# The MLP of an encoder layer: earlier loads for the background sums, one more set of output buffers, a finish with other spacing

## The chip, the core and the metric

One core of one Trainium2 chip runs the whole layer. The metric is the device time of one execution in microseconds (us); for the kernel before, the median of three runs is 3302.6 us (3301.38 to 3305.57). The engines are TensorE (PE), VectorE (DVE), ScalarE (ACT), GpSimd (POOL) and SyncE (SP), which issues nearly all DMAs of this part.

## The reference, cut to what matters

The layer works on `x` of 2048 tokens by 1024 channels, all in float32: an SSD (Mamba-2) head group and a windowed attention group, mixed by `w_out`, and then the MLP, which is the part that the change touches:

```python
x = x + rmsnorm(mix, norm_mix_post[i])
h = rmsnorm(x, norm_mlp_pre[i])                             # 2048 x 1024
f = jnp.square(jax.nn.relu(h @ w_up[i])) @ w_down[i]        # 1024 -> 4096 -> 1024
x = x + rmsnorm(f, norm_mlp_post[i])
```

## The kernel before

**Precision.** A float32 product is made of three matmuls: each operand is split into a high part (ACT rounds a copy) and a low part (DVE or POOL subtracts the copy), and hi*hi, hi*lo and lo*hi are summed in PSUM. A weight or input that reaches PE thus costs one ACT copy and one subtraction.

**Fast products.** The two large products of the MLP use a 2x2 block scheme with seven block products in place of eight. For this the operands are needed in linear combinations: sums of input blocks, sums of weight blocks, and sums of the outputs of the first product, which are the inputs of the second.

**Up.** The tokens go in two halves (`hf` 0 and 1). Each half has 16 steps `p`; a step makes seven products (`PROD` = 1, 5, 6, 3, 7, 2, 4) of 12 matmuls of 128x512 each, into PSUM tiles psmx, psmy and psmz. Products 1, 5, 6 and 4 are copied by ACT into SBUF tiles `c` (L1083; product 4 with a ReLU, L1054), products 3, 7 and 2 are added to them by DVE (L1086). Product 3 goes on accumulating in the bank of product 5, and product 7 in that of product 6, so PE can start them only when ACT has copied the bank out. The `c` tiles have five buffers (tag "ct") for four tiles a step. At the end of a step POOL forms four more combinations (L1096, L1098, L1100, L1105) in tiles `t`, and all of it is stored to DRAM (`dop`). The last four steps of the second half store to `dff` and need no combinations.

**Inputs of up.** `up_input` loads the rows of `x2`, scales them, forms the combinations on DVE and POOL, and splits them (L1039, L1040) into tiles of the pools "u" (16) and "a" (16). For the second half it starts in step 15 of the first, each set when the set of the first half that it replaces has been used.

**Weights of down.** In the background, `w_sums` takes 16 jobs: load four tiles of `w_down` into the four buffers of the tag "nt" (L1117), four additions on POOL in place (L1121), four stores to `dws` (L1122). It starts after step 3 of the first half. The tag "nt" also holds the scratch tiles of `rnorm` and `rsqrt`, which `r2` calls at step 8 of each half, when PE has summed the squares (`ssq`).

**Down.** `down_fast` runs four quarters for the first half of the tokens and three for the second, 28 products of 12 matmuls each; the last quarter goes as an ordinary product (`down`). `down_weights` loads `wd` tiles and splits them (L1147, L1148); `down_input` brings the inputs back from `dop` through the small staging tiles "gl" (2) and "ld" (3), and splits them (L1164, L1165). The tags "ld" and "gl" also hold POOL's `t` tiles. `finals` finishes the first half of the tokens while the second runs: one `ssq` on PE for each of two column blocks, then eight times a scale, an addition and a store (L1281 to L1285).

**Order of the work.** The order on PE is the order in which the program is written: generators are interleaved by a clock `self.t` that counts matmul time, 512/2400 of a microsecond for each 128x512 matmul (17.92 units a step of up), and `yield n` means "not before n units from now". On the other engines a scheduler orders the instructions when the program is built; there the place in the program is a priority, and a tile's buffer is given out in program order.

Of the kernel before, what the change touches and what calls it, by code (L numbers as in the profile page):

```python
# [37 lines left out]
class Layer:  # L38
    def __init__(self, ctx, tc, a, out):
# [21 lines left out]
        self.d_x2 = d("dx2", [8, P, T])  # L61
        self.d_h = d("dh", [2, 8, P, 2, 2, TB])
# [901 lines left out]

    def up_weights(self):
# [11 lines left out]
        for u in range(32):  # L977
            nxt = load((u + 1) % 16) if u < 31 else None
            for m in self.PROD:
# [5 lines left out]
                w = self.wp.tile([P, 2, 4, P], F32R, tag="ws", name="ws", bufs=4)  # L985
                nc.scalar.copy(w[:, 0], x)  # L986
                self.eng("wlo").tensor_sub(w[:, 1], x, w[:, 0].bitcast(F32))  # L987
                yield w
# [8 lines left out]
    def up_input(self, hf, B):  # L997
# [5 lines left out]
        sets = ((("raw1", "u", None), ("raw2", "u", None), (1, "u", None), (5, "u", None), (6, "a", "ws10"),  # L1003
                 (3, "a", "ws10"), (7, "a", "ws11"), (2, "a", "ws11"), (4, "u", None)) if hf == 0 else
                (("raw1", "u", None), ("raw2", "u", "uA1"), (1, "u", "uA5"), (5, "a", "uA6"), (6, "a", "uA3"),
                 (3, "a", "uA7"), (7, "a", "uA2"), (2, "u", "uA4"), (4, "u", None)))
        x = {}

        def raw(b, tag):

            x[b] = []
            for i in range(4):
                t = self.unit(tag, "x2", F32)
                for k in range(2):
                    kt = 4 * k + i
                    nc.sync.dma_start(t[:, k], self.d_x2[kt, :, self.tok(hf, b - 1)])
# [7 lines left out]
        for s, tag, after in sets:  # L1024
            if after:
                yield self.until(after)
            if s in ("raw1", "raw2"):
                yield self.until(f"x2_{hf}{int(s[3]) - 1}")
# [14 lines left out]
            self.flags.add(f"B{hf}{s}")  # L1043

    def up(self, hf, p, B, ws):
# [15 lines left out]
        for m in self.PROD:  # L1061
# [16 lines left out]
            if m in (1, 5, 6, 4):  # L1078
                c[m] = self.pw.tile([P, TB], F32, tag="ct", name=f"c{m}", bufs=5)
# [28 lines left out]
    def w_sums(self):  # L1108

        nc = self.nc  # L1110
        for qt in range(4):
            for p in range(4):
                a = {}
                for i in range(2):
                    for k in range(2):
                        t = a[f"{i + 1}{k + 1}"] = self.nt("wsum")
                        nc.sync.dma_start(t.rearrange("p (k c) -> p k c", k=4), self.a["w_down"][2 * p + i, 2 * qt + k])  # L1117
                yield 6
                for m, fn, x, y, o in ((5, "tensor_add", "21", "22", "21"), (6, "tensor_sub", "21", "11", "11"),
                                       (7, "tensor_sub", "22", "11", "22"), (3, "tensor_sub", "12", "11", "12")):  # L1120
                    getattr(nc.gpsimd, fn)(a[o], a[x], a[y])  # L1121
                    nc.sync.dma_start(self.d_ws[(5, 6, 7, 3).index(m), qt, p], a[o])  # L1122
                yield 22
# [8 lines left out]
    def down_weights(self):  # L1132
        nc = self.nc
        for hf in range(2):
            for qt in range(3 if hf else 4):
                for m, ps in self.DPH:
                    for p in ps[::2]:
                        raw = self.pf.tile([P, 2, 4, P], F32, tag="f", name="wd", bufs=8)
# [6 lines left out]
                        for x in range(2):  # L1145
                            w = self.wp.tile([P, 2, 4, P], F32R, tag="ws", name="ws", bufs=4)
                            nc.scalar.copy(w[:, 0], raw[:, x])  # L1147
                            self.eng("wlo").tensor_sub(w[:, 1], raw[:, x], w[:, 0].bitcast(F32))  # L1148
                            yield w

    def down_input(self):

        nc = self.nc
        done = ["uB5", "uB6", "uB3", "uB7"]
        for hf in range(2):
            for qt in range(3 if hf else 4):
                for m in self.DIN:
                    yield self.until(done.pop(0))
                    done.append(f"D{hf}{qt}{m}")
                    B = self.B2[hf, qt, m] = []  # L1160
                    for i in range(4):
                        x = self.stage(self.d_op[hf, m - 1, 4 * qt + i], i)
                        t = self.slot("ff")
# [417 lines left out]
```

## Time and profile before

| | us |
|---|---|
| median of three runs | 3302.6 |
| the profiled execution | 3297.75 |
| its span | 3296.0 |
| PE busy in the span | 2973.0 (90%) |
| DVE, ACT, POOL busy | 2167.4, 1555.7, 1132.7 |
| DMA, mean rate | 179 GB/s |

The MLP takes the last 45% of the span. A busy PE counts its pipelined matmuls, and a stretch at the lower granted clock is also busy, so idle time of PE and its granted clock are read together. Idle time of the other engines costs nothing by itself.

### The profile page before, as it was taken

The numbers are of one execution on the slowest core, as the hardware profiler recorded it, in microseconds if no ns is written. First come the engines' busy times: TensorE is split into PE (matmuls) and PEld (weight loads), VectorE is DVE, ScalarE is ACT, GpSimd is POOL, SyncE is SP. The second block draws the span as 40 slices with busy tenths as digits, with TensorE's granted clock in tenths as the row PEclk, the third lists the DMA queues.
The fourth block names the chain that finished last, engine by engine and source line by source line (L and its number), as shares of the span: only waits on it lengthen the run. The fifth ranks groups of instructions, "written<-read, shape, count | busy, mean of one in ns | idle before, by whom it ended". The sixth has DMA issues, their size and how long they took to land. (4 is left out here: it accounts for less than half of the span.)

```text
span 3296.0 us, 40950 instructions
## 1 busy us (share of the span) xinstructions
PE 2973.0 (90%) x13560; PEld 2369.2 (72%) x13560; DVE 2167.4 (66%) x3514; ACT 1555.7 (47%) x2886; POOL 1132.7 (34%) x900
## 2 busy tenths in 40 slices
PE   7989999999998899997978779886998899988996
PEld 6878887778876666674756557764877788877886
DVE  7365555557757788859778855648564467767766
ACT  3235566667765445222132535534554554454432
POOL 4242222222233444654536555567344000020001
PEclk9999999999999999997989989988999999999998
DMA  6767544475568645655257465564445556557633
GB/s 227 238 201 202 147 126 119 125 215 136 154 210 258 194 140 157 186 172 160 88 165 242 161 229 185 210 221 171 148 165 205 188 188 201 194 178 249 193 104 97
DMA packets 422117, 589.19 MB, mean 179 GB/s; under 512 B 34704, under 2 KB 202640, under 8 KB 421904
## 3 DMA queue, kind: packets, MB, share of 16 engines
q1 hardware_dynamic: 387280, 550.90, 54.0%
q10 hardware_dynamic: 34624, 35.66, 3.1%
q8 instruction: 108, 1.77, 0.2%
q14 instruction: 105, 0.86, 0.1%
HBM read 391.77 MB, written 194.65 MB: 178 GB/s over the span
## 5 line engine op out<-in xcount | busy, mean ns | idle before, releaser
L88 PE MATMUL psg<-h,ws 128*128 128x512 f32 x1920 | 486.4, 400 | 19.3 <-ACT z L472 17.9
L88 PEld LDWEIGHTS psg<-h,ws 128*128 128x128 f32 x1920 | 356.9, 190 | 93.0 <-issue 18.6
L220 POOL TENSOR_SCALAR ws<-wr 128x512 fp32r<-128x512 f32 x184 | 126.6, 688 | 740.7 <-PE psg L88 602.3
L86 PE MATMUL psmx<-b,ws 128*128 128x512 f32 x1152 | 304.1, 415 | 41.1 <-ACT c L1083 19.4
L86 PEld LDWEIGHTS psmx<-b,ws 128*128 128x128 f32 x1152 | 229.5, 201 | 101.1 <-ACT c L1083 22.6
L223 POOL TENSOR_TENSOR ws<-wr,ws 128x512 fp32r<-128x512 f32 x184 | 250.7, 1363 | 14.7
L88 PE MATMUL psg<-hr,ws 128*128 128x512 f32 x960 | 248.6, 399 | 5.0 <-DMA hr<-dh 4.3
L779 DVE CUSTOM_DVE_ANT_0 p<-psqk,pack,sinks 128x384 f32<-128x384 f32 (+1 forms) x256 | 151.9, 596 | 139.3 <-PE psqk L88 138.6
L86 PE MATMUL psx<-ff,ws 128*128 128x512 f32 x1008 | 233.9, 392 | 7.8 <-DVE ws L1148 7.7
L88 PE MATMUL psg<-ga,ws 128*128 128x512 f32 x768 | 209.9, 426 | 26.4 <-DVE mix L895 11.8
L86 PEld LDWEIGHTS psx<-ff,ws 128*128 128x128 f32 x1008 | 190.4, 189 | 49.1 <-DVE ws L1148 9.1
L1147 ACT CAST ws<-wd 128x512 fp32r<-128x512 f32 x196 | 121.9, 623 | 215.4 <-PE psx L86 93.4
L88 PE MATMUL psg<-ya,ws 128*128 128x512 f32 x768 | 212.9, 418 | 2.0 <-DVE ya L203 1.9
L88 PEld LDWEIGHTS psg<-hr,ws 128*128 128x128 f32 x960 | 175.9, 189 | 41.7 <-DMA hr<-dh 7.1
L88 PEld LDWEIGHTS psg<-ga,ws 128*128 128x128 f32 x768 | 150.6, 201 | 75.1 <-issue 11.9
L88 PEld LDWEIGHTS psg<-ya,ws 128*128 128x128 f32 x768 | 142.0, 193 | 43.4 <-issue 15.0
L987 DVE TENSOR_TENSOR ws<-wc,ws 128x512 fp32r<-128x512 f32 x128 | 132.8, 1039 | 56.4 <-ACT ws L986 56.0
L790 ACT ACTIVATE p<-p,m 128x384 f32<-128x384 f32 (+1 forms) x256 | 150.9, 591 | 35.3 <-DVE m L785 35.1
L208 ACT CAST pt<-pspt 128x512 fp32r<-128x512 f32 x184 | 107.0, 583 | 119.2 <-PE pspt L92 103.4
L1148 DVE TENSOR_TENSOR ws<-wd,ws 128x512 fp32r<-128x512 f32 x196 | 137.1, 701 | 38.1 <-ACT ws L1147 37.8
L209 DVE TENSOR_TENSOR pt<-pspt,pt 128x512 fp32r<-128x512 f32 x184 | 125.5, 684 | 50.2 <-ACT pt L208 49.7
L88 PE MATMUL psy<-ff,ws 128*128 128x512 f32 x672 | 156.7, 390 | 1.7 <-DVE facc L1205 1.2
(246 smaller groups left out, 6455.2 us busy)
## 6 DMA issues: line engine op xcount, KB each, us to landing
stg<-dop SPq DMA_DIRECT2D x196, 256.0 KB, 3.5
wu<-w_up_dram SPq DMA_DIRECT2D x128, 256.0 KB, 3.3
wr<-w_in_dram SPq DMA_DIRECT2D x120, 256.0 KB, 2.8
dop<-c SPq DMA_DIRECT2D x112, 256.0 KB, 2.3
wd<-dws SPq DMA_DIRECT2D x56, 512.0 KB, 4.2
k<-dk SPq DMA_DIRECT2D x56, 384.0 KB, 4.8
dop<-t SPq DMA_DIRECT2D x84, 256.0 KB, 2.1
wd<-w_down_dram SPq DMA_DIRECT2D x42, 512.0 KB, 4.3
```

The costliest lines, as they stand in the source:

```text
L86: self.nc.tensor.matmul(out, lhsT, rhs, start=False, stop=stop, skip_group_check=True)
L88: self.nc.tensor.matmul(out, lhsT, rhs, start=start, stop=stop)
L208: self.nc.scalar.copy(hi, src)
L209: self.nc.vector.tensor_sub(lo, src, hi.bitcast(F32))
L220: self.nc.gpsimd.tensor_scalar(w[:, 0], raw, 1.0, 0.0, ALU.mult, ALU.add)
L223: eng.tensor_sub(w[:, 1], raw, w[:, 0].bitcast(F32))
L779: nc.vector.tensor_tensor_reduce(out=p[:, :W], in0=ps[:, :W], in1=bias, scale=1.0, scalar=self.sinks[:, hd:hd + 1], op0=ALU.add, op1=ALU.m ...
L790: nc.scalar.activation(p4[r][:, :W], p4[r][:, :W], AF.Exp, bias=m[:, 0, r:r + 1], scale=float(np.float32(SLOPES[hd])), accum_out=m[:, 2, r ...
L987: self.eng("wlo").tensor_sub(w[:, 1], x, w[:, 0].bitcast(F32))
L1147: nc.scalar.copy(w[:, 0], raw[:, x])
L1148: self.eng("wlo").tensor_sub(w[:, 1], raw[:, x], w[:, 0].bitcast(F32))
```

## The change

- `w_sums` becomes `sums`: 20 jobs in place of 16. The first four jobs load four tiles of `x2` of the second half, scale them, and store the seven inputs of the second half's up products to a new DRAM array `dxo`. Then come the 16 jobs on `w_down`. The loads of a job are written three units behind the sums of the job before, and its sums 18 units later (before: loads, 6 units, sums, 22 units).
- `up_input1` replaces `up_input` for the second half: it loads the ready inputs through the staging tiles and only splits them, from step 14 on.
- The `c` tile of product 4 goes to the tag "wr" (two buffers of the weight chunks, not in use during up); the five "ct" buffers serve the other three.
- The first four `wd` tiles go to "nt" buffers, as part of a weight stream that starts in the last step of up; `down_input` starts in step 14 with its first set in the "u" pool.
- `finals` starts 8 units later, and its elements are 7 units apart (before: 1.5). The same `yield` serves the first of the three last parts.

```diff
+    def up_input1(self, B):
+        for m, tag, after in ((1, "u", "xo"), (5, "u", "uA1"), (6, "u", "uA5"), (3, "a", "uA6"), (7, "a", "uA3"),
+                              (2, "a", "uA7"), (4, "a", "uA2")):
+            yield self.until(after)
+            B[m] = []
+            for i in range(4):
+                x = self.stage(self.d_xo[m - 1, i], i)
+                t = self.unit(tag, "b")
+                nc.scalar.copy(t[:, 0], x)
+                self.eng("flo").tensor_sub(t[:, 1], x, t[:, 0].bitcast(F32))
+                B[m].append(t)
+                yield 1.0
+            self.flags.add(f"B1{m}")
...
-                c[m] = self.pw.tile([P, TB], F32, tag="ct", name=f"c{m}", bufs=5)
+                c[m] = (self.wp.tile([P, TB], F32, tag="wr", name="c4", bufs=2) if m == 4 else
+                        self.pw.tile([P, TB], F32, tag="ct", name=f"c{m}", bufs=5))
...
+    def sums(self):
+        def load(job):
+            a = {}
+            for i in range(2):
+                for k in range(2):
+                    t = a[f"{i + 1}{k + 1}"] = self.nt("sum")
...
+        def x_sums(i, a):
+            for y, m in (("11", 1), ("12", None), ("22", 3), ("21", 2)):
+                kt = 4 * int(y[0]) - 4 + i
+                nc.vector.tensor_scalar(a[y], a[y], vec[:, kt:kt + 1], None, ALU.mult)
+                if m:
+                    nc.sync.dma_start(self.d_xo[m - 1, i], a[y])
+            t1, t2 = self.ld(name="t1"), self.gl("t2")
+            nc.gpsimd.tensor_sub(t1, a["12"], a["11"])
+            nc.sync.dma_start(self.d_xo[4, i], t1)
+            nc.gpsimd.tensor_sub(t2, a["22"], t1)
+            nc.sync.dma_start(self.d_xo[5, i], t2)
+            nc.gpsimd.tensor_sub(a["12"], a["22"], a["12"])
+            nc.sync.dma_start(self.d_xo[6, i], a["12"])
+            t4 = self.ld(name="t4")
+            nc.gpsimd.tensor_sub(t4, a["21"], t2)
+            nc.sync.dma_start(self.d_xo[3, i], t4)
...
+        jobs = [(i,) for i in range(4)] + [(qt, p) for qt in range(4) for p in range(4)]
+        a = load(jobs[0])
+        for n, job in enumerate(jobs):
+            yield 18
+            (x_sums if len(job) == 1 else w_sums)(*job, a)
+            if n == 3:
+                self.flags.add("xo")
+            elif n > 3 and job[1] == 3:
+                self.flags.add(f"sum{job[0]}")
+            if n + 1 < len(jobs):
+                yield 3
+                a = load(jobs[n + 1])
...
+                        if (hf, qt, m) == (0, 0, 1):
+                            raw = [self.nt("wd").rearrange("p (k c) -> p k c", k=4) for _ in range(2)]
+                            for x in range(2):
+                                nc.sync.dma_start(raw[x], self.a["w_down"][2 * (p + x), 0])
+                                yield self.wsplit(raw[x])
+                            continue
...
-        done = ["uB5", "uB6", "uB3", "uB7"]
+        done = [None, "uB3", "uB7", "uB2", "uB4"]
...
+        yield self.until(f"sum{qt}")
...
-            yield 0 if xs else 1.5
+            yield 0 if xs else 7
...
+                if (hf, p) == (1, 15):
+                    ws = itertools.chain(ws, self.down_weights())
...
-                if p == 15:
-                    if hf == 0:
-                        self.side(self.up_input(1, B[1]))
-                    else:
-                        self.side(self.down_input())
+                if p == 14:
+                    self.side(self.down_input() if hf else self.up_input1(B[1]))
...
-                self.side(self.finals(both, facc, facs))
+                self.side(self.finals(both, facc, facs), 8)
```

## Rows read from the trace of the kernel before

**Rows 1.** Windows: stretch, length, busy PE, PEld, DVE, ACT, POOL; PEclk, DMA, GB/s.

```profile
1821.76:1957.16 135.40, 93.54 (x341) 71.83 (x340) 94.33 (x111) 63.58 (x108) 63.20 (x41) 0.86 0.58 192
1957.16:2069.12 111.96, 103.06 (x425) 82.38 (x424) 63.84 (x70) 58.84 (x96) 57.73 (x39) 0.95 0.53 183
2069.12:2246.24 177.12, 144.49 (x590) 116.01 (x589) 96.20 (x104) 76.71 (x133) 108.27 (x74) 0.90 0.64 228
2246.24:2295.58 49.34, 28.92 (x85) 18.89 (x84) 45.70 (x35) 21.59 (x40) 44.40 (x29) 0.77 0.35 122
2295.58:2429.25 133.67, 133.67 (x590) 110.64 (x588) 81.02 (x92) 74.88 (x127) 56.40 (x39) 1.00 0.44 156
2429.25:2524.28 95.03, 82.14 (x341) 65.52 (x340) 51.13 (x60) 49.48 (x80) 47.54 (x34) 0.95 0.58 199
...
2611.54:2922.31 310.77, 307.56 (x1344) 254.04 (x1345) 212.41 (x318) 149.89 (x252) 19.14 (x14) 0.99 0.61 195
2922.31:3173.97 251.66, 236.71 (x1012) 191.87 (x1013) 184.81 (x282) 121.01 (x203) 12.17 (x8) 0.98 0.65 204
```

**Rows 2.** Timeline of PE, an undisturbed step: start, length, line, output, count.

```profile
2339.49 2.88 PE L86 MATMUL psmx<-b,ws 128*128 128x512 f32 x12
2342.21 2.88 PE L86 MATMUL psmy<-b,ws 128*128 128x512 f32 x12
```

**Rows 3.** Waits of PE, 1957 to 2246: total us, times, longest.

```profile
PE psmy L86 <- ACT c L1083: 28.6, 8, 11.8
PE psmx L86 <- DVE c L1086: 6.6, 1, 6.6
PE ssq L88 <- DMA xsld<-dxs: 3.3, 1, 3.3
```

**Rows 4.** Waits of ACT, 1957 to 2246.

```profile
ACT c L1083 <- POOL c L1100: 52.7, 9, 15.5
```

**Rows 5.** Waits of POOL, 1957 to 2246.

```profile
POOL wsum L1121 <- DMA wsum<-w_down_dram: 53.9, 7, 9.6
```

**Rows 6.** Timeline of POOL: sums of a job before and after each gap.

```profile
2001.22 6.49 POOL L1121 TENSOR_TENSOR wsum<-wsum 128x512 f32<-128x512 f32 x4 [6.56 <-DMA wsum<-w_down_dram]
...
2079.57 6.39 POOL L1121 TENSOR_TENSOR wsum<-wsum 128x512 f32<-128x512 f32 x4
...
2287.32 1.73 POOL L1121 TENSOR_TENSOR wsum<-wsum 128x512 f32<-128x512 f32 x1
...
2465.51 6.40 POOL L1121 TENSOR_TENSOR wsum<-wsum 128x512 f32<-128x512 f32 x4
```

**Rows 7.** Timeline of PE: the first `ssq` of `r2` in each half.

```profile
2053.30 1.43 PE L88 MATMUL ssq<-xsld,ones 128*128 128x512 f32 x2 [3.29 <-DMA xsld<-dxs]
...
2438.97 1.39 PE L88 MATMUL ssq<-xsld,ones 128*128 128x512 f32 x2 [2.76 <-DMA xsld<-dxs]
```

**Rows 8.** Line L1121 and loads L1117: durations ns (min/median/max); landing time.

```profile
L1121 POOL TENSOR_TENSOR wsum<-wsum x64: 1261/1622/1813, 1957.3 to 2506.5; 128x512 f32<-128x512 f32 x64
...
DMA to landing us min/median/max: 2.6/4.1/6.8
```

**Rows 9.** Subtractions on DVE: with POOL at work (L1040), without (L1165).

```profile
L1040 DVE TENSOR_TENSOR b<-x,b x14: 678/1748/1780, 2238.1 to 2292.4; 128x512 fp32r<-128x512 f32 x14
...
L1165 DVE TENSOR_TENSOR ff<-stg,ff x75: 679/691/694, 2940.5 to 3132.0; 128x512 fp32r<-128x512 f32 x75
```

**Rows 10.** Timeline of PE: the longest stall of steps 0 to 3.

```profile
1908.36 5.49 PE L86 MATMUL psmy<-b,ws 128*128 128x512 f32 x12 [11.35 <-ACT c L1083]
```

**Rows 11.** Timeline of PE: the start of down.

```profile
2611.54 13.81 PE L88 MATMUL psx<-ff,ws 128*128 128x512 f32 x48 [10.94 <-ACT ws L1147]
```

**Rows 12.** Timeline of PE at the change of halves; waits of SP, 2900 to 3020.

```profile
2922.31 1.13 PE L88 MATMUL ssq<-facs,ones 128*128 128x512 f32 x2 [3.21 <-POOL facs L911]
...
2981.47 5.04 PE L86 MATMUL psx<-ff,ws 128*128 128x512 f32 x12 [6.80 <-DVE ws L1148]
...
SPq L1285 <- POOL facc L1284: 23.7, 8, 4.9
```

More of the change, by code (lines that the diff above doesn't have):

```diff
@@ L1 @@
+import itertools
 from contextlib import ExitStack
@@ L963, in combine, with wsplit @@
         return out
+    def wsplit(self, x):
+        w = self.wp.tile([P, 2, 4, P], F32R, tag="ws", name="ws", bufs=4)
+        self.nc.scalar.copy(w[:, 0], x)
+        self.eng("wlo").tensor_sub(w[:, 1], x, w[:, 0].bitcast(F32))
+        return w
     def up_weights(self):
@@ L984, in up_weights @@
                                               self.pw.tile([P, 4, P], F32, tag="cmb", name="wc", bufs=3))
[L985 to L988, printed above, removed]
+                yield self.wsplit(x)
             raw = nxt
@@ L995, in unit, with up_input @@
         return self.pu.tile([P, 2, TB], dt, tag="u", name=name, bufs=16)
-    def up_input(self, hf, B):
+    def up_input1(self, B):
+        nc = self.nc
+        for m, tag, after in ((1, "u", "xo"), (5, "u", "uA1"), (6, "u", "uA5"), (3, "a", "uA6"), (7, "a", "uA3"),
[10 more added lines that the diff above has]
+            self.flags.add(f"B1{m}")
+    def up_input(self, B):
         nc = self.nc
         w = self.vec["norm_mlp_pre"]
[L1003 to L1006, printed above, removed]
+        sets = (("raw1", "u", None), ("raw2", "u", None), (1, "u", None), (5, "u", None), (6, "a", "ws10"),
+                (3, "a", "ws10"), (7, "a", "ws11"), (2, "a", "ws11"), (4, "u", None))
         x = {}
@@ L1027, in up_input @@
             if s in ("raw1", "raw2"):
-                yield self.until(f"x2_{hf}{int(s[3]) - 1}")
+                yield self.until(f"x2_0{int(s[3]) - 1}")
                 yield from raw(int(s[3]), tag)
@@ L1145, in down_weights @@
                         for x in range(2):
[L1146 to L1149, printed above, removed]
+                            yield self.wsplit(raw[:, x])
     def down_input(self):
         nc = self.nc
-        done = ["uB5", "uB6", "uB3", "uB7"]
+        done = [None, "uB3", "uB7", "uB2", "uB4"]
         for hf in range(2):
@@ L1157, in down_input @@
                 for m in self.DIN:
-                    yield self.until(done.pop(0))
-                    done.append(f"D{hf}{qt}{m}")
+                    after = done.pop(0)
+                    if after:
+                        yield self.until(after)
+                        done.append(f"D{hf}{qt}{m}")
                     B = self.B2[hf, qt, m] = []
@@ L1162, in down_input @@
                         x = self.stage(self.d_op[hf, m - 1, 4 * qt + i], i)
-                        t = self.slot("ff")
+                        t = self.unit("a" if after else "u", "ff")
                         nc.scalar.copy(t[:, 0], x)
@@ L1468, in main @@
                     s3.close()
-                    self.side(self.w_sums())
+                    self.side(self.sums())
         self.worder = [("w_down", j, (6, 7)) for j in range(8)]
```

36 lines of the change are left out of this document (17 added, 19 removed).

## The prediction

> **What bounds the kernel now.** I read the windows first, cut at the starts of up's steps, then the timeline of PE for the price of undisturbed work, then who made PE wait, and whom that engine waited for.
>
> An undisturbed product starts 2.72 us after the one before [rows 2], so a step of up takes 7 x 2.72 = 19.04 us and a quarter of down 28 x 2.72 = 76.16 us. Against this, the stretches lose [rows 1]: steps 0 to 3 of the first half 135.4 - 76.2 = 59.2 us; steps 4 to 8 112.0 - 95.2 = 16.8; steps 9 to 15 177.1 - 133.3 = 43.8; step 0 of the second half 49.3 - 19.0 = 30.3; steps 1 to 7 133.7 - 133.3 = 0.4; steps 8 to 11 95.0 - 76.2 = 18.8. Down starts with a wait of 10.94 us, and its first 48 matmuls take 13.81 us where four products take 11.04: 13.7 lost [rows 11]. The first half of down loses 3.2 more at its end [rows 12], and the three quarters of the second half 251.7 - 228.5 = 23.2. In all some 209 us. PE sets the time of the MLP; what can be won is its idle time and what the lower clock adds behind each stall (the granted clock is 0.77 to 0.90 in the losing stretches, 1.00 where nothing is lost).
>
> In steps 4 to 15 the waits sum to some 41 us, 28.6 of them for ACT's copy out of psmy in eight stalls [rows 3]; the loss of 60.6 is 1.46 times the waits, which is the price of the clock. ACT in turn waited for a free `c` buffer, released by L1100 on POOL [rows 4], and POOL had stood idle in front of the background sums, for loads that had not landed [rows 5]. The jobs of those sums do not run evenly: three up to 2008, none until 2080, ten up to 2289, none until 2465, the last three after that [rows 6]. The gaps end behind the `ssq` of `r2` [rows 7]: its scratch tiles are in the same four buffers and come first in the program. So the jobs run as fast as the buffers turn round, far ahead of their place, until they meet `r2`. The stalls lie where jobs run; steps 1 to 7 of the second half have no jobs and lose nothing.
>
> **The change part by part.**
>
> *Loads one step ahead.* The four buffers still hold one job. The loads of the next cannot start before the stores of this one have left, whatever the program says, and where jobs already run ahead, the new order takes little from the 53.9 us that POOL waits [rows 5]. I count no gain here; the other end, all such waits gone, is a rival. Twenty jobs are distributed anew: the four on `x2` stay near their place, as their `t` tiles share buffers with up's; then jobs 4 to 17 come before the second `r2`, fourteen in place of ten. At 22 us a job (ten in 2069 to 2289) eight of them fall before the end of the first half, as many with the first four as now, and six spill over into steps 0 to 6 of the second.
>
> *Output buffers.* Now product 5's tile has to wait for L1100, and PE wants it copied when product 3 begins. With five buffers for three tiles a step, product 5 finds a free one, and the first to wait is product 6, wanted when product 7 begins: one product later, 2.72 us. The eight stalls behind psmy are 0.68, 2.85, 0.34, 7.64, 1.12, 1.27, 11.80 and 2.85 us (sum 28.6 [rows 3]); each gives up at most 2.72, in all 14.3. The stall of 6.6 us on DVE in step 15 comes with the old input and shrinks to 2. With the clock: (14.3 + 4.6) x 1.46 = 27.6. Against it `r2` finds its scratch tiles taken by the last job on `x2`: ACT then stands in front of it, and copies out of PSUM queue behind. That costs between nothing and one job's four sums (4 x 1.62 = 6.5 [rows 8]); I take 3.6. Steps 4 to 15: **-24** (-48 to +5).
>
> Steps 0 to 3 are held by `post`, unchanged. Only the stall of 11.35 us [rows 10], where a `c` copy stands behind `post` on ACT, can use a buffer earlier: **-8** (-20 to +5).
>
> The six jobs that spill over cost what twelve cost after the change in steps 4 to 15, 14.3 x 1.46 / 12 = 1.7 us each: **+10** in steps 1 to 7 (0 to +28, at the old 60.6 / 13 = 4.7 each). In steps 8 to 11 two jobs remain of three (3.4 us), and `r2` keeps its wait of 2.8 [rows 7], which with the clock and its own matmuls makes 6.4: 18.8 becomes 10, **-9** (-13 to +3).
>
> *Input of the second half.* The 16 scalings and the combinations leave this place, and 14 subtractions move from POOL to DVE. The first set is loaded in step 14. The other 24 tiles have from the end of product 1 in step 15 to product 4 of step 0, 19.04 + 16.32 - 2.72 = 32.6 us. DVE is busy for 81.0 of 133.7 us in undisturbed steps [rows 1], so 12.8 us are free. A subtraction costs 0.69 us where POOL is quiet and 1.75 at the median where it works [rows 9]: 24 cost 16.6 to 42 us, 3.8 to 29 too much. POOL works less than now but runs six jobs here; I take 1.1 us, 26.4 in all, 13.6 short, with the clock 15. Step 0 falls from 30.3 to 15: **-15** (-27 to +10).
>
> The Trainium skill's page "SBUF — State Buffer", section "SBUF: two separate sides", says that DVE with two SBUF inputs and GpSimd take their shared port as an exclusive lock. The 0.69 and 1.75 us agree. Taken strictly it speaks against the change, as every subtraction would meet a POOL operation: that is the weak rival below, with a sum of -26 in place of -76.
>
> *First weights.* Loaded to "nt" buffers that have been free since the sums ended, they remove the wait and the slow start: 13.7 becomes 1.7, **-12** (-13.7 to -5). The next set of `wd` still waits for up's memory, but has 10.9 us more.
>
> *Finish.* Now 16 elements come in a burst; SP stands 23.7 us before stores that wait for POOL, and the loads for down queue behind it [rows 12]. Spread over 112 units plus 8, the burst is gone, and `ssq` no longer stands in front of PE. Its work stays: DVE, busy for 184.8 of 251.7 us [rows 1], and POOL. Of 3.2 + 23.2 = 26.4 I leave 8: **-18** (-24 to -5). The first of the last parts now spreads 8 elements over 56 units, while the remaining matmuls take 41: two elements are written behind the end. The engines are idle there: **0** (0 to two elements of two DVE operations, 4 x 0.69 = +2.8).
>
> *At nothing:* `sum` and `xo` only order the program (the last job is written before step 12); down's first set is loaded a step earlier, in buffers that no one waits for; 28 stores and 12 more loads lie under matmuls, at a DMA share of 0.65 at most where PE works [rows 1]; should that cover go, they are late tiles, inside the bounds above.
>
> Sum: -24 - 8 + 10 - 9 - 15 - 12 - 18 = **-76**. The profiled execution took 3297.75 us; 3221.75 after. The median is 4.85 above that execution: 3226.6, so 3227 us.
>
> **The rivals.**
>
> *Strong: the loads do come early.* POOL waits no more for them. For: in undisturbed steps POOL has half its time free. Against: the four buffers. Steps 4 to 15 keep `r2` and a little (-46), steps 1 to 7 stay clean, steps 8 to 11 -12, step 0 -22, the rest -10 - 13 - 22: -125, 3178 us.
>
> *Weak: only the transitions are won.* Each subtraction meets POOL: 24 x 1.75 = 42 us, step 0 stays at 29 (-1); the spilled jobs cost 4.7 each (+28); steps 4 to 15 -14, the rest -8 - 9 - 12 - 10: -26, 3277 us. The words "one step ahead" would then describe nothing that happens. For: rows 9. Against: POOL loses 14 subtractions in just that place.
>
> *Slower: the staging buffers starve the second half.* The new inputs come through five small buffers, and up's `t` tiles hold up to three of them until POOL is done and the store has left. A round of one buffer is 4.1 us of landing [rows 8] plus copy and subtraction, some 5.4. With one buffer, 24 tiles take 130 us, 97 more than there is: step 0 loses 97 in place of 30.3, +67, against -61 from the rest: +6, 3309 us, and the second `r2` and the jobs behind it come late on top. It turns slower than before at about (32.6 + 30.3 + 61) / 24 = 5.2 us a tile; five buffers give 1.1, two 2.7. Against: the `t` tiles hold three of the five only for a part of each step.
>
> **How the numbers follow.** Forecast 0.59 (its own range 3200 to 3258), strong 0.17, weak 0.16, slower 0.08. 0.2% is 6.6 us, about what a measurement of this kernel can tell from no change: faster 0.90 (the first three but for 0.02 of the weak case), within 0.03 (those 0.02, and 0.01 of the slower case), slower 0.07. The range of 8 in 10 takes in most of the strong and nearly all of the weak case: 3180 to 3279.
>
> **What would show it.** Right: psmy's waits for ACT down to about half; jobs in a run from `r2` into step 6 of the second half, with POOL still waiting for their loads; 10 to 20 us lost in step 0, on DVE's subtractions; no wait above 3 us at the start of down; no stall above 4 us behind the finish, with SP's waits for POOL there under 10 us. Wrong: POOL's waits for loads gone (strong); step 0 still losing 30 us or more, with DVE subtractions near 1.75 us (weak) or SP standing for staging buffers (slower).

## The result and the profile after

The changed kernel takes 3279.06 us (median of four runs, 3278.06 to 3280.41) against 3301.99 us of the kernel before in the same session (3299.38 to 3305.57): ratio 0.993, 95% interval 0.9913 to 0.9947. It is faster by 23 us, or 0.7%; 76 us were forecast, and the time lies just above the upper end of the range.

The windows of the kernel after, cut at the starts of the same steps as [rows 1] (same columns); line numbers in a row are those of the kernel that ran, so in the changed kernel L1103 is the copy that was L1083, L1106 the addition that was L1086, L1116 to L1125 POOL's combinations, L1150 the scaling of `x2` and L1167 the additions of the jobs on `w_down`.

```profile
1824.25:1951.29 127.04, 92.94 (x341) 72.14 (x340) 93.45 (x103) 62.85 (x108) 61.72 (x40) 0.88 0.52 170
1951.29:2074.62 123.33, 105.55 (x425) 83.92 (x424) 69.30 (x87) 58.09 (x97) 62.86 (x43) 0.93 0.66 225
2074.62:2253.16 178.54, 148.06 (x590) 119.06 (x588) 90.24 (x106) 80.18 (x140) 99.11 (x69) 0.89 0.66 229
2253.16:2283.35 30.19, 23.11 (x86) 15.00 (x84) 22.91 (x30) 19.29 (x35) 12.43 (x9) 1.00 0.81 274
2283.35:2426.12 142.77, 136.61 (x589) 111.59 (x588) 81.11 (x90) 73.59 (x126) 72.29 (x52) 0.98 0.56 193
2426.12:2516.62 90.50, 82.59 (x341) 65.44 (x340) 53.41 (x60) 48.21 (x80) 47.86 (x34) 0.96 0.61 210
2516.62:2604.82 88.20, 78.19 (x337) 64.28 (x336) 44.13 (x61) 48.64 (x85) 15.88 (x11) 0.94 0.45 156
...
2604.82:2909.46 304.64, 304.64 (x1345) 252.09 (x1344) 215.74 (x321) 153.22 (x261) 16.92 (x13) 1.00 0.66 212
2909.46:3157.30 247.84, 236.95 (x1015) 192.79 (x1014) 184.87 (x281) 118.53 (x201) 15.16 (x10) 0.98 0.63 204
```

Length less 19.04 us a step of up and 76.16 us a quarter of down gives what each stretch loses, as in the prediction:

| stretch | lost before | lost after | forecast | measured |
|---|---|---|---|---|
| steps 0 to 3 | 59.2 | 50.9 | -8 | -8.3 |
| steps 4 to 8 | 16.8 | 28.1 | -24 with the next | +11.3 |
| steps 9 to 15 | 43.8 | 45.3 | | +1.5 |
| second half, step 0 | 30.3 | 11.2 | -15 | -19.1 |
| steps 1 to 7 | 0.4 | 9.5 | +10 | +9.1 |
| steps 8 to 11 | 18.8 | 14.3 | -9 | -4.5 |
| steps 12 to 15 | 0 | 12.0 | 0 | +12.0 |
| start of down | 13.7 | 0 | -12 | -13.7 |
| rest of down before the last parts | 26.4 | 19.3 | -18 | -7.1 |
| sum | 209.4 | 190.6 | -76 | -18.8 |

(The two profiled executions, 3297.75 and 3280.41 us, differ by 17.3 us, partly because up starts 2.5 us later in the second; neither is the median of its kernel, and the medians differ by 23.) Five terms came within 5 us of the forecast. Three did not: steps 4 to 15, 36.8 us off; step 12 of the second half, 12 us; the finish, 10.9 us.

The waits of the kernel after in steps 4 to 15 (1951 to 2253 us), which answer to [rows 3 to 5]: engine, line, what it waited for, total us, times, longest.

```profile
PE psmx L88 <- ACT c L1103: 27.8, 6, 10.5
PE psmx L88 <- DVE c L1106: 15.7, 4, 5.5
PE psmy L88 <- ACT c L1103: 3.2, 1, 3.2
...
ACT c L1103 <- POOL c L1120: 30.3, 5, 14.2
...
POOL sum L1167 <- DMA sum<-w_down_dram: 53.0, 7, 11.6
...
DVE sum L1150 <- DMA sum<-dx: 25.5, 7, 7.2
```

The 28.6 us behind psmy are gone but for 3.2, and 27.8 us now stand behind psmx: the same chain, one product later. POOL's wait for loads is what it was, 53.0 us after 53.9. New is DVE, which waits for the loads of `x2`. The timeline of the kernel after shows one such chain from end to end (start, length, instruction, idle time before it and its releaser); POOL first, then ACT, then PE:

```profile
2161.62 5.95 POOL L1167 TENSOR_TENSOR sum<-sum 128x512 f32<-128x512 f32 x4 [6.55 <-DMA sum<-w_down_dram]
2175.05 1.26 POOL L1167 TENSOR_TENSOR sum<-sum 128x512 f32<-128x512 f32 x1 [7.48 <-DMA wu<-w_up_dram]
...
2177.49 1.27 POOL L1116 TENSOR_TENSOR t<-c,c 128x512 f32<-128x512 f32 x1
2178.71 1.71 POOL L1167 TENSOR_TENSOR sum<-sum 128x512 f32<-128x512 f32 x1
2180.38 1.71 POOL L1118 TENSOR_TENSOR t<-c,t 128x512 f32<-128x512 f32 x1
2182.05 1.71 POOL L1120 TENSOR_TENSOR c<-c,c 128x512 f32<-128x512 f32 x1
...
2183.79 0.59 ACT L1103 COPY c<-psmx 128x512 f32<-128x512 f32 x1 [14.17 <-POOL c L1120]
...
2184.42 5.49 PE L88 MATMUL psmx<-b,ws 128*128 128x512 f32 x12 [10.51 <-ACT c L1103]
```

Two jobs follow each other within 14 us. POOL stands 6.55 us for the loads of the first and 7.48 us before the second (the row puts the end of that wait down to a load of `w_up`; SP issued the second job's own four loads from 2167.97 on, behind the first job's stores). The step's own combinations L1116 to L1120, which free the `c` buffer for ACT, come behind. What the stall costs beyond its 10.5 us is in the last row: 12 matmuls take 5.49 us where those of an undisturbed product take 2.88 [rows 2].

The new stall in step 12 of the second half: POOL, SP, ACT and PE (the first set of down's input is SP's L199 and ACT's L1226):

```profile
2515.27 5.99 POOL L1167 TENSOR_TENSOR sum<-sum 128x512 f32<-128x512 f32 x4 [5.89 <-DMA sum<-w_down_dram]
...
2530.91 0.32 SPq L1079 DMA_DIRECT2D dop<-t  x1
2531.28 2.77 SPq L199 DMA_DIRECT2D stg<-dop  x4
...
2535.84 1.30 ACT L1226 CAST ff<-stg 128x512 fp32r<-128x512 f32 x2 [12.48 <-DMA stg<-dop]
...
2537.68 4.75 PE L88 MATMUL psmx<-b,ws 128*128 128x512 f32 x12 [10.01 <-ACT c L1103]
```

The last job's additions run across the start of step 12 (2516.62), the combinations of step 11 follow them on POOL, and SP issues the set's four loads right behind the last store of those combinations, 14.7 us into the step. ACT has by then stood before the first copy since 2523.36.

The split of the second half's input, by line (min, median and longest in ns), and the four stalls left in down:

```profile
L1013 DVE TENSOR_TENSOR b<-stg,b x28: 680/688/1765, 2216.4 to 2281.0; 128x512 fp32r<-128x512 f32 x28
...
2933.55 5.74 PE L90 MATMUL psy<-ff,ws 128*128 128x512 f32 x24 [1.08 <-ACT facc L1266]
2942.43 5.74 PE L88 MATMUL psy<-ff,ws 128*128 128x512 f32 x24 [3.14 <-ACT facc L1266]
...
2979.04 8.58 PE L90 MATMUL psy<-ff,ws 128*128 128x512 f32 x24 [3.67 <-DVE facc L1268]
...
3018.48 7.33 PE L88 MATMUL psy<-ff,ws 128*128 128x512 f32 x24 [2.77 <-DVE facc L1268]
```

### The profile page after: what moved, and what is told of

The parts are those of the page before. It is cut to its first block, busy times and chain, and to the rows that moved or that the text cites. A ratio compares the mean times of both kernels' runs of the same rounds, so it can differ in the third digit from the quotient of the medians.

```text
span 3278.6 us, 41081 instructions
## 1 busy us (share of the span) xinstructions
PE 2977.4 (91%) x13560; PEld 2374.7 (72%) x13560; DVE 2149.8 (66%) x3517; ACT 1551.4 (47%) x2886; POOL 1116.6 (34%) x897
## 5 line engine op out<-in xcount | busy, mean ns | idle before, releaser
L90 PE MATMUL psg<-h,ws 128*128 128x512 f32 x1920 | 486.4, 399 | 19.3 <-ACT z L474 17.9
L88 PE MATMUL psmx<-b,ws 128*128 128x512 f32 x1152 | 319.2, 430 | 95.4 <-ACT c L1103 64.3
L88 PEld LDWEIGHTS psmx<-b,ws 128*128 128x128 f32 x1152 | 237.4, 209 | 163.4 <-ACT c L1103 71.0
L225 POOL TENSOR_TENSOR ws<-wr,ws 128x512 fp32r<-128x512 f32 x184 | 250.0, 1359 | 14.7
L970 DVE TENSOR_TENSOR ws<-wc,ws 128x512 fp32r<-128x512 f32 x128 | 124.7, 976 | 68.6 <-ACT ws L969 68.3
L211 DVE TENSOR_TENSOR pt<-pspt,pt 128x512 fp32r<-128x512 f32 x184 | 125.5, 684 | 49.8 <-ACT pt L210 49.3
```

The costliest lines, as they stand in the source:

```text
L88: self.nc.tensor.matmul(out, lhsT, rhs, start=False, stop=stop, skip_group_check=True)
L90: self.nc.tensor.matmul(out, lhsT, rhs, start=start, stop=stop)
L211: self.nc.vector.tensor_sub(lo, src, hi.bitcast(F32))
L225: eng.tensor_sub(w[:, 1], raw, w[:, 0].bitcast(F32))
```

## The experiments

Each time is a median, with its ratio to the kernel before on the same chip and the 95% interval. The groups of runs were on different chips, so kernels of different groups are compared by their ratios. Losses are those of the table's stretches.

### Parts of the change alone

**The output buffer alone, in the kernel before** (`c4` to "wr"):

```diff
-                c[m] = self.pw.tile([P, TB], F32, tag="ct", name=f"c{m}", bufs=5)
+                c[m] = (self.wp.tile([P, TB], F32, tag="wr", name="c4", bufs=2) if m == 4 else
+                        self.pw.tile([P, TB], F32, tag="ct", name=f"c{m}", bufs=5))
```

> The kernel before with one edit: the c tile of product 4 moves to the weight-chunk buffers, so five buffers serve three c tiles a step. Theory A (the prediction's step): each stall behind ACT's copies in steps 4 to 15 gives up one product, 2.72 us, and steps 0 to 3 win 8: some 25 to 35 us less in all, 3267 to 3277 us, psmy's waits for ACT in steps 4 to 15 falling from 28.6 to about 14. Theory B (POOL stands for the loads of the background sums, and the wait only passes on to the next product that needs a buffer): psmy's waits vanish and psmx's appear with nearly the same sum, 25 us or more; only steps 0 to 3 win: 3290 to 3297 us.

3292.58 us, 0.9974 (0.9958 to 0.9989). Steps 0 to 3 lose 49.8 in place of 59.2; steps 4 to 8 lose 18.9 and steps 9 to 15 lose 43.9, no less than before. The window of steps 9 to 15, and then PE's waits in steps 4 to 15 (1954 to 2246):

```profile
2068.18:2245.36 177.18, 142.83 (x590) 115.13 (x589) 92.55 (x105) 76.76 (x135) 107.39 (x74) 0.92 0.65 228
```

```profile
PE psmx L86 <- ACT c L1084: 30.1, 6, 11.9
...
PE psmy L86 <- ACT c L1084: 3.2, 2, 2.4
```

177.18 us, where it was 177.12 [rows 1], and the 28.6 us behind psmy [rows 3] have become 30.1 us behind psmx. The buffer helps where one copy is a little late behind `post`; where POOL itself is late it only decides which product waits.

**The first weights of down alone, in the kernel before** (in "nt" buffers, as part of a stream that starts in the last step of up):

```diff
+                        if (hf, qt, m) == (0, 0, 1):
+                            raw = [self.nt("wd").rearrange("p (k c) -> p k c", k=4) for _ in range(2)]
...
+                if (hf, p) == (1, 15):
+                    ws = itertools.chain(ws, self.down_weights())
```

> The kernel before with one edit: the first four down weights go to the nt buffers in a stream that starts in the last step of up. Both theories: the 10.9 us wait at the start of down and the slow start after it go, 12 to 14 us less, 3288 to 3290 us, and nothing else moves.

3291.47 us, 0.9971 (0.9956 to 0.9986): the 11.1 us lost at the end of up fall to 0.0, as both expected; the time falls by 11.2 us, a little under the 12 to 14 of the expectation.

**The finish alone, in the kernel before:**

```diff
-            yield 0 if xs else 1.5
+            yield 0 if xs else 7
...
-                self.side(self.finals(both, facc, facs))
+                self.side(self.finals(both, facc, facs), 8)
```

> The kernel before with one edit: the finish starts 8 units later and its elements are 7 units apart. Theory A (the burst and SP behind it made the loss of 26): 15 to 20 us less, 3282 to 3287 us. Theory B (each element still puts DVE and SP in front of something that has not come; spreading only spreads it): 5 to 9 us less, 3293 to 3297 us, with waits of PE for facc still there.

3292.99 us, 0.9974 (0.9962 to 0.9987). Down before its last parts loses 23.3 in place of 29.5 (slow start included): -6.2, a third of the -18 forecast. (The execution in the profile is the slowest of the ten, 3302.95 us: up starts 13.5 us later in it than in that of the kernel before, ahead of all that the edit touches.) Four stalls of 1.0 to 4.2 us behind the copies and additions of `facc` are there already.

**The change without the new way of the second half's input**: `up_input(1, ...)` as before from step 15, and only the 16 weight jobs, in the new order:

```diff
-        jobs = [(i,) for i in range(4)] + [(qt, p) for qt in range(4) for p in range(4)]
+        jobs = [(qt, p) for qt in range(4) for p in range(4)]
...
-                if p == 14:
-                    self.side(self.down_input() if hf else self.up_input1(B[1]))
+                if p == (14 if hf else 15):
+                    self.side(self.down_input() if hf else self.up_input(1, B[1]))
```

> The kernel after, but the second half's input is made as before (no sums on x2, up_input in step 15), and the sums have their 16 jobs on w_down in the new order. Theory B (the x jobs put DVE in front of loads in steps 4 to 8, and push six jobs into the second half): steps 4 to 8 lose 17 us or less again in place of 28, steps 1 to 7 of the second half lose nothing, step 0 loses 30 again: the sum is within 8 us of the kernel after, 3271 to 3287 us. Theory A (the new input route is worth its 15 to 19 us, and what it costs elsewhere is small): 15 us or more slower than after, 3294 us or more.

3268.07 us, 0.9901 (0.9881 to 0.992), below both expected ranges, and a larger gain than that of the whole change (0.993, 0.9913 to 0.9947; the intervals just overlap). Step 0 of the second half loses 28.7 again, but steps 4 to 8 lose 21.1 in place of 28.1, steps 1 to 7 0.4 in place of 9.5, steps 8 to 11 6.3 in place of 14.3, steps 12 to 15 1.7 in place of 12.0. The four jobs on `x2` win 17 us in step 0 and cost more than that elsewhere. Steps 9 to 15 keep 43.0 us: that loss does not come from them.

### What holds steps 4 to 15

**The scaling of `x2` on POOL** (L1150, changed kernel):

```diff
-                nc.vector.tensor_scalar(a[y], a[y], vec[:, kt:kt + 1], None, ALU.mult)
+                nc.gpsimd.tensor_scalar(a[y], a[y], vec[:, kt:kt + 1], None, ALU.mult)
```

> The kernel after with one edit: the 16 scalings of the x2 tiles in the background jobs run on POOL in place of DVE. Theory B (in steps 4 to 8 DVE stands in front of x2 loads that have not landed, 22 us, and the additions out of PSUM behind it hold PE for 15.7): those waits of PE for DVE go; POOL stands for the loads instead, which costs part of it again: steps 4 to 8 lose 16 to 22 us in place of 28, the time falls by 5 to 12 us, 3267 to 3274. Rival (the sixteen scalings and their 28 stores simply are more work): no change, 3277 to 3281, or more.

3282.54 us, 0.9944 (0.9927 to 0.9961); steps 4 to 8 lose 29.3. POOL waits for the same loads in DVE's place (waits of POOL, 1950 to 2080; then PE in the same steps):

```profile
POOL sum L1150 <- DMA sum<-dx: 14.6, 4, 4.9
...
2060.42 2.07 PE L90 MATMUL ssq<-xsld,ones 128*128 128x512 f32 x2 [15.15 <-DMA xsld<-dxs]
```

The stand before the loads goes with the instruction to the other engine. PE's waits for DVE in these steps do go, from 15.7 us to 1.5, as the theory says, but another comes in their place: the `ssq` of `r2` waits 15.15 us for its input, where it waited 0.9. So the gain did not come. What made that load late was not tried.

**Half-size jobs, really loaded one ahead** (on the kernel without the four `x2` jobs: 32 jobs of two tiles; two jobs share the four buffers, and the next job's loads are written ahead of this one's sums):

```diff
-            yield 18
-            (x_sums if len(job) == 1 else w_sums)(*job, a)
+            nxt = load(jobs[n + 1]) if n + 1 < len(jobs) else None
+            yield 10.5
+            w_sums(*job, a)
+            a = nxt
```

> The kernel e4 (after, but the second half's input as before) with the jobs on w_down cut in halves of 256 columns, two buffers each, so that the loads of one half-job really run while the one before is summed (32 half-jobs, 128 shorter additions). The strong rival of the prediction: POOL's waits for loads fall to less than a third, steps 9 to 15 lose 20 us or less in place of 43: 3248 us or below. Theory B in the form that only the distance between the planned and the real landing counts: the jobs only run denser, POOL still stands for the loads, steps 9 to 15 lose 35 us or more: 3262 to 3280 us.

3267.34 us, 0.9901 (0.9881 to 0.9921), the same as without it. POOL's waits for loads fall from 80.9 to 37.0 us, not to the third that was expected, and steps 9 to 15 lose 41.2 (43.0). POOL also has a wait that the kernel with whole jobs does not have, for stores of the jobs' own tiles (waits of POOL, 1950 to 2600):

```profile
POOL sum L1131 <- DMA sum<-w_down_dram: 37.0, 16, 6.1
POOL sum L1131 <- DMA dws<-sum: 22.1, 5, 7.4
```

So 59 of the 81 us of waiting remain. Loads written earlier won nothing, and this is as near to the "strong" rival of the prediction as was built; but POOL's stand did not go away in it, so the run can't tell what its absence would win.

**The changed kernel without the 64 additions of the weight jobs** (it leaves out the sums themselves, and stores the tiles as loaded; loads and stores stay):

```diff
-                getattr(nc.gpsimd, fn)(a[o], a[x], a[y])
```

> The kernel after without the four POOL additions of the 16 jobs on w_down (the loaded tiles are stored as they are, so the down product is not computed from the right sums). Loads and stores stay. Theory B (POOL stands in front of loads of those jobs, and its own combinations, and by them ACT's copies, come late): steps 9 to 15 lose under 15 us in place of 45, steps 1 to 7 nothing, steps 8 to 11 only r2's 6: 40 us or more less, 3240 us or below. Rival (the traffic of the jobs on SP and the DMA engines is what makes things late): steps 9 to 15 still lose 30 us or more, 3265 us or above.

3215.22 us, 0.9742 (0.9722 to 0.9762). Steps 9 to 15:

```profile
2069.30:2205.76 136.46, 134.11 (x589) 110.13 (x588) 84.39 (x104) 79.16 (x138) 54.21 (x37) 1.00 0.94 324
```

They lose 3.2 us, at a DMA share of 0.94 and 324 GB/s. Steps 12 to 15 of the second half lose 1.2, while steps 4 to 8 keep 26.6. So DMA traffic is not what holds steps 9 to 15; the jobs' additions, with the waits before them, are: 32 of the 64 are in this stretch (69 instructions of POOL against 37), and 45 us of its busy time. Two readings are left: POOL has too much work, or its work stands in the wrong place.

**Jobs kept at their place.** The reading to test was the second: the scheduler may take up a job as soon as the four "nt" buffers are free, and nothing else holds it. In the next three kernels the first of a job's four sums goes to an `ld` tile, a buffer that the steps themselves use and that is given out in program order:

```diff
+            s5 = self.ld(name="s5")
+            nc.gpsimd.tensor_add(s5, a["21"], a["22"])
+            nc.sync.dma_start(self.d_ws[0, qt, p], s5)
+            for m, x, y, o in ((6, s5, "11", "11"), (7, a["22"], "11", "22"), (3, a["12"], "11", "12")):
+                nc.gpsimd.tensor_sub(a[o], x, a[y])
...
```

Without the `x2` jobs:

> The changed kernel with the second half's input made as before (as e4), and one more edit: the first of a job's four sums is written to an `ld` tile, a buffer that the steps themselves use in program order, in place of one of the job's own load buffers. A job then can't be taken up before its place in the program. Theory (the jobs run ahead of their place as fast as their buffers turn, and POOL stands before loads that have not landed): POOL's waits for loads, 81 us in the changed kernel, fall under 25; steps 9 to 15 lose 10 to 20 us in place of 43, steps 8 to 11 of the second half 5 to 10, step 0 stays at 25 to 30; 3225 to 3245 us (3268 without the edit). Rival (POOL's work itself is too much for these steps, wherever the jobs stand): steps 9 to 15 keep 35 us or more, or the same loss moves to steps 1 to 7 of the second half; 3260 to 3275 us.

3233.50 us, 0.9799 (0.978 to 0.9819), against 0.9901 without the edit. Steps 9 to 15 lose 9.0 us in place of 43.0, a little less than expected, and POOL waits for no load of a job any more (80.9 us without the edit).

In the whole changed kernel:

> The changed kernel, whole, with the one edit of g1: the first of each of the 16 weight jobs' sums goes to an `ld` tile. Theory: steps 9 to 15 lose 10 to 20 us in place of 45, steps 1 to 7 of the second half under 5 in place of 9.5, step 12 of the second half nothing in place of 12 (its late staging buffers hang on POOL as well), while steps 4 to 8 keep their 28, as the jobs on the input are not touched: 3279 - 30 - 6 - 11 = about 3232, 3220 to 3245 us. Rival: as in g1, less than 10 us in all, 3268 to 3280 us.

3246.49 us, 0.9828 (0.9808 to 0.9849), against 0.993. Its steps 9 to 15:

```profile
2077.60:2223.11 145.51, 138.08 (x590) 113.08 (x588) 98.92 (x106) 80.31 (x140) 86.98 (x58) 0.97 0.68 242
```

12.2 us lost in place of 45.3, and 2.5 in place of 9.5 in steps 1 to 7 of the second half. A miss: steps 12 to 15 still lose 11.0, where nothing was expected, and the time lies just above the expected range.

And in the kernel before, with nothing else changed:

> The kernel before with one edit: the first of each weight job's four sums goes to an `ld` tile in place of one of the job's own load buffers, so that no job is taken up before its place in the program. Theory (half or more of what steps 9 to 15 lost before was POOL's stand before loads of jobs taken up too early): these steps lose 10 to 20 us in place of 43.8, and what is left of the jobs falls on steps 1 to 7 of the second half without loss over 5 us; 3302 - 25 - 30 = 3270 to 3285 us. Rival (before the change the wait for a free `c` buffer was due to the amount of POOL's work in these steps): under 10 us less, 3292 to 3303 us.

3249.32 us, 0.9846 (0.983 to 0.9862): this one edit gains more than twice what the whole change gained, and more than expected. Its steps 9 to 15, and then ACT's wait of [rows 4] in it, 1957 to 2235:

```profile
2072.86:2216.41 143.55, 136.64 (x590) 111.85 (x588) 98.88 (x106) 77.35 (x135) 93.58 (x62) 0.98 0.68 237
```

```profile
ACT c L1083 <- POOL c L1100: 16.9, 6, 3.9
```

10.3 us lost in place of 43.8; ACT's wait falls from 52.7 to 16.9. POOL is busy for 65% of this stretch, more than in [rows 1] (61%), so a share as high as before does not make the loss. The sixteen jobs now start between 1973 and 2481, at most 69 us apart, and POOL never waits for their loads. The rival (under 10 us less) falls. Two things changed together, though: POOL no longer stands, and five jobs run in these steps in place of eight; three moved on to later steps, and steps 1 to 7 of the second half lose only 1.3 us with five jobs in them. The edit also gives a job one more buffer, which no run separates from the order.

The gain is larger than expected because other stretches with jobs win too: steps 4 to 8 lose 11.2 in place of 16.8, step 0 of the second half 20.4 in place of 30.3, steps 8 to 11 8.0 in place of 18.8.

**The additions out of PSUM free of the wait for `x2`** (the paced kernel, with the `x2` jobs rewritten: the first scaling into an `ld` tile, the others in one chain on DVE that starts from it, three operations on POOL):

```diff
+            nc.vector.tensor_scalar(t1, a["11"], u, None, ALU.mult)
...
+            nc.vector.scalar_tensor_tensor(a["12"], a["12"], u, t1, ALU.mult, ALU.subtract)
...
+            nc.vector.scalar_tensor_tensor(a["22"], a["22"], v, a["12"], ALU.mult, ALU.subtract)
...
```

> g2, with the jobs on the input written in another way: the scaled first quadrant goes to an `ld` tile, the other scalings and subtractions are one chain of three operations on DVE that begins from it, and POOL keeps three. DVE's operations on the input then can't be taken up before the steps' own `ld` tiles come free, in place of standing 22 us before loads with the additions out of PSUM behind them. Theory (DVE's stand before the input's loads is what made steps 4 to 8 dearer, 28 us in place of 17): these steps fall to 12 to 20 us, the rest as g2; 8 to 16 us less than g2. Rival (what steps 4 to 8 lose comes from POOL and the buffers that the `t` tiles share, whoever scales): within 5 us of g2.

3231.77 us, 0.979 (0.9772 to 0.9809). Steps 4 to 8 lose 17.7 in place of 30.7, DVE's waits for `x2` are gone from its list, and PE's waits for DVE fall from 14.2 us to 3.3. So the new 11 us of steps 4 to 8 came with DVE's stand before loads. (The rewriting also takes one of four operations of each such job from POOL, which is not separated.)

### What holds step 12 of the second half

**The first set's copies on POOL** (changed kernel):

```diff
-                        nc.scalar.copy(t[:, 0], x)
+                        if after:
+                            nc.scalar.copy(t[:, 0], x)
+                        else:
+                            nc.gpsimd.tensor_scalar(t[:, 0], x, 1.0, 0.0, ALU.mult, ALU.add)
```

> The kernel after with one edit: the high parts of down_input's first set are rounded by POOL (idle in steps 12 to 15 of the second half) in place of ACT. Theory B (the scheduler puts ACT's copies of this set before a copy out of PSUM in step 12, and ACT stands 12.5 us for the staging loads): the 10.0 us wait of PE in step 12 goes, 8 to 12 us less, 3267 to 3271. Rival (the wait is for a c buffer or for SP, and ACT only shows it): step 12 still loses 8 us or more, 3276 to 3281.

3274.08 us, 0.9923 (0.9902 to 0.9943). The stretch still loses 11.5 us; ACT now waits for stores of `c` tiles instead (waits of ACT, 2480 to 2560):

```profile
ACT c L1103 <- DMA dop<-c: 10.7, 2, 6.5
```

**The first set called for in step 15** (on the paced kernel with the chain), and then **held back by a flag** until product 1 of step 15 is done:

```diff
-                if p == 14:
+                if p == 14 + hf:
```

> g3, with down's first set of input called for in step 15 of the second half, as in the kernel before, in place of step 14. Theory (the set's four loads queue on SP behind the stores of the last job and land late, and ACT stands before them with the copies out of PSUM behind it): the 10.5 us that steps 12 to 15 lose fall under 3, down starts without a wait over 3 us, 8 to 10 us less than g3, 3218 to 3226 us. Rival (the set is late wherever it is called for, and the wait moves into step 15 or to the start of down): within 4 us of g3, 3226 to 3238 us.

```diff
-                    if after:
-                        yield self.until(after)
+                    yield self.until(after or "uB1")
+                    if after:
```

> g3, with the first set of down's input held back by a flag until product 1 of step 15 of the second half is done, as in the kernel before; h1 moved only the call, and the set came no later. Theory (the set's loads beside the last job's loads and stores make the copies of it late, and the additions out of PSUM stand behind them): steps 12 to 15 lose under 3 us in place of 10.5 to 12.3, and down starts without a wait over 3 us; 8 to 10 us less than g3's 3231.8, 3219 to 3226 us. Rival (the last job alone makes the stall, or the set is late in step 15 too): within 4 us of g3.

3232.47 us, 0.9782 (0.9766 to 0.9799), and 3237.99 us, 0.9816 (0.9798 to 0.9833): no gain from either. Steps 12 to 15 lose 12.3 and 10.9 us. But neither did what it was meant to: SP issues the set's first load at the same place, in step 12, as it did at 2485.70 without either edit (first row the later call, then the flag):

```profile
2485.51 0.43 SPq L199 DMA_DIRECT2D stg<-dop  x1
```

```profile
2488.03 0.43 SPq L199 DMA_DIRECT2D stg<-dop  x1
```

The set's place in the program and a flag moved nothing here. Why the scheduler takes it up there was not tried.

**The last job sooner** (the paced kernel with the chain, 14 units in place of 18 between a job's loads and its sums):

```diff
-            yield 18
+            yield 14
```

> g3, with 14 in place of 18 units of the planner between a job's loads and its sums, so that the last of the 20 jobs comes some four steps earlier; down's first set stays where it is. Theory (the set is late only because the last job's loads and stores are in SP's queue and on the DMA engines with it): steps 12 to 15 lose under 3 us in place of 10.5; the jobs stand closer, which costs 0 to 10 us in steps 4 to 15, where each job's loads have less time to land; 3220 to 3232 us. Rival (the set is late by itself): the 10 to 12 us stay, 3230 to 3242 us.

3229.54 us, 0.9783 (0.9764 to 0.9803). Steps 12 to 15 lose 1.2 in place of 10.5; the set's four loads are issued together, again in step 12, 7.0 us into the step (14.7 in the changed kernel), with no store or load of a job beside them:

```profile
2476.34 1.87 SPq L199 DMA_DIRECT2D stg<-dop  x4
```

So the stall comes from the first set and the last job meeting, not from the set alone. The kernels without the `x2` jobs, whose last job also comes earlier, say the same: 1.7 us above, and 1.2 with the jobs kept at their place. Step 0 of the second half loses 22.1 in place of 17.2, and the time itself is not told apart from the kernel without this edit. With 0.979 and 0.9782 above it is among the fastest of the kernels that compute the whole layer: 2.2% under the kernel before, 1.5% under the changed one.

## Why the prediction was wrong

**The step that failed is "Output buffers", the -24 for steps 4 to 15.** The prediction took up to 2.72 us and its clock off each of eight stalls because the first product to wait comes one later. That holds only if the copy's release stays where it was. Here it came from POOL, for which ACT stood up to 15.5 us [rows 4], and the wait passed on: the stalls went from psmy to psmx, and steps 4 to 15 lost 12.8 us more in place of 24 less, 1.5 of it in steps 9 to 15 (45.3 after 43.8). The buffer alone shows it without the rest of the change: 30.1 us behind psmx for 28.6 behind psmy.

**The cause was in the prediction's own reading.** It says that the jobs run "far ahead of their place" and that "the stalls lie where jobs run", and then counted no gain from loads one ahead, which holds (POOL waits 53.0 us for them after 53.9). What it did not ask is what the running ahead costs. With jobs held to their places the same rows, 43.8 us, shrink to 10.3 in the kernel before. Late loads are how the cost shows, since POOL stands in front of them; half-size jobs halved the waits for loads, put 22.1 us of waits for stores beside them, and lost as much. How the loss divides between POOL's standing, the jobs' coming first and the number of jobs in these steps stays open.

**Not named: DVE's new stand.** The 16 scalings of `x2` were moved to DVE "near their place", at nothing. They wait for loads, 25.5 us in seven waits, with the additions out of PSUM behind them: 11.3 us more are lost in steps 4 to 8, 28.1 in all, and 17.7 with the chain in the paced kernel.

**"At nothing: down's first set is loaded a step earlier"** cost 12.0 us. ACT waits for its loads, and SP issues these behind stores that wait for POOL. The prediction placed six jobs in steps 0 to 6 of the second half and two after `r2`; four and four came, so the last one ran into step 12, where it met the set. "Late tiles, inside the bounds above" was the right danger, without a place or a price.

**The finish was mis-sized.** The loss at the change of halves is gone (3.2 before, 0 after). But spreading only spread SP's stand for POOL's additions, which the prediction wanted under 10 us: 17.8 us in the stretch of [rows 12], and 24.8 over the whole finish, after 23.7. Four stalls behind the copies and additions of the accumulators remain; 19.3 is lost where 8 was taken. Alone the edit gave -6.2. What releases these four stalls was not tried.

**Right, by their own steps:** steps 0 to 3 (-8.3 for -8, and -9.4 from the buffer alone), and the first weights of down (-13.7 for -12; alone -11.1 at the end of up).

**Near in number, by other steps.** The spill into steps 1 to 7 cost 9.1 for 10, but with four jobs at 2.3 us in place of six at 1.7. Step 0 of the second half won 19.1 for 15. The sum let DVE run short of time there, at 1.1 us a subtraction, and raised its 13.6 us to 15 for the clock, where the factor 1.46 that it uses elsewhere gives 19.9. In the run the subtractions took 0.69 us at the median, as POOL was busy there for only 12.4 of 30.2 us, and the round of the staging buffers set the pace (waits of ACT and of SP, 2236 to 2284):

```profile
ACT b L1012 <- DMA stg<-dxo: 11.7, 10, 4.9
...
SPq L199 <- DVE b L1013: 10.9, 13, 1.7
```

SP stands before a load until a subtraction has freed the staging tile, and ACT stands for the load. That is the mechanism of the "slower" rival, at 11.2 us lost in this step in place of 97.

The Trainium skill's page "SBUF — State Buffer", section "SBUF: two separate sides", says that DVE with two SBUF inputs and GpSimd take the shared port as an exclusive lock. The prediction's weak rival took from it that every subtraction would meet POOL; the median of 0.69 us says that few did. The trace agrees with the lock where they met: the longest of the 28, 1765 ns, lies beside POOL's L1116 to L1120. Of the rivals, the weak one was nearest in time (3277), but for another reason: the transitions were won, and the loss lay in the steps between.

One reading of the prediction is narrower than its rows: the granted clock of losing stretches goes up to 0.95, in steps 4 to 8 and 8 to 11, and not to 0.90 [rows 1].

## What to carry to other kernels

Where background work shares an engine with the work that sets the time, ask first what holds it at its place: here a buffer given out in program order did for the jobs, while loads written earlier did not, and for down's first set neither a later call nor a flag did. A free buffer behind a late engine moved a stall here and did not shorten it, so follow the wait to the engine that released it and past that to what that engine stood for. Before pricing a change of a background stream, price its present place: one buffer was worth 49 us here, the change 23.

## What the runs showed that was not expected

Without the additions the same loads and stores ran at 324 GB/s and a DMA share of 0.94 through seven steps, with PE at a granted clock of 1.00 and only 3.2 us lost: at this rate the transfers themselves cost PE almost nothing, where the same jobs with their additions had cost 45.3.
